# One ring over the attention stage's three PSUM banks and five new ones, and a gain's preparation held back, in a Griffin-style layer on one core

## The chip, the core and the metric

The kernel runs on one core of one Trainium2 chip, as a single launch. The metric is the device time of one execution in microseconds. Before the change it is 1303.85 us, the median of three runs (1301.6 to 1304.78).

## The reference

One layer: a mixer that adds stick-breaking attention and a short gated convolution under two sigmoid gates, and then a convolutional feed-forward network. Both have an RMS norm ahead of them and one behind them. The sequence has 1024 positions, the model 1024 channels, the feed-forward 2816.

```python
h = rms_norm(x, norm_mix_pre)
proj = h @ w_in
q, k, v, cb, cc, cx, g_att, g_conv = jnp.split(proj, IN_SPLITS, axis=-1)
o = stick_breaking_attention(heads(q), heads(k), heads(v))      # 8 heads of 64
y_att = o @ w_att_branch
y_conv = (cb * causal_dwconv(cc * cx, conv_mix_w)) @ w_conv_branch
merged = sigmoid(g_att) * y_att + sigmoid(g_conv) * y_conv
x = x + rms_norm(merged @ w_out, norm_mix_post)

h = rms_norm(x, norm_ffn_pre)
u = causal_dwconv(h @ w_up, conv_ffn_w)
a, g = jnp.split(u, 2, axis=-1)
x = x + rms_norm((gelu(g) * a) @ w_down, norm_ffn_post)
```

## The kernel before

All products are made in half precision with float32 sums. Each operand is split into a high and a low half (L102 on ScalarE writes the high one, L103 on VectorE the low one), and each product is three passes over the pairs of halves. Weights are scaled by a power of two first: ScalarE squares a raw tile and sums it (L63, the `jk_` names), TensorE adds over the partitions with a column of ones (L81, L1419, `pr`), and a few small VectorE steps make the scale from that (L83 to L86, L1414 to L1417).

The layer runs in stages, and each PSUM product takes a bank of a pool:

- **Attention** (to about 407 us), in an order written by hand. Its pools hold eight banks: `pm`, three, for projections and branch products, and a pool of its own for scores and outputs. Branch products made here (`pywc`, L935) are emptied on VectorE by L943.
- **Branches and gates** (410 to 597 us). Attention's pools are closed, and a pool `pz` of eight banks is opened over the same memory. Products of the branches (`pywc`, `pywa`) alternate with those of the gates, one pair of gates per block of 128 channels, d from 1 to 7. A pair is made of seven half-size products in three banks, `pg{d}a`, `pg{d}b` and `pg{d}c` (`Pair.prod`, L2333): several products go one after the other into one bank, and the later ones can only start when the earlier content has been copied out (L2348 and L2353 on ScalarE, L2350, L2357, L2360 and L2362 on VectorE, results `ca`, `cg` and `ug`). The merged activations `ywa` (L1217, L1219) are split into `m16_0` to `m16_7`. In between come loads and squares of `w_down` (`ds`, `jk_dn`: L1314 and L63) and the fetch and split of the next gate's weights (`ws_g`, `wh_g`) and of `w_out` (`ws_wo`, `wh_wo`). The order of this stage on each engine isn't written by hand: it comes from the program's scheduling pass, which knows the pools' banks.
- **Feed-forward** (`ffn`, from about 597 us). Here a planner writes the order of all engines: each step has an engine, a cost, the buffers that it reads and writes and sometimes a due time, and a buffer's `avail` is the planner's time from which steps that touch it may start. The stage begins with the output projection (`py`, L1482: eight tiles of 128 positions in two halves), its norm (L1492 to L1506), the residual, the next norm (L1511) and the transposes (`pt`, L1570). The up-projection follows (L1681, `pu`).

The vector `g_ffn` is the gain of the second norm. It arrives by a DMA at the end of the gates; `gain()` then takes its largest magnitude over the 1024 channels (L1455), makes a power of two of it in four small steps (L199 to L202), and L1458 scales the vector. Before, these steps are ready as soon as the load is. Sums over partitions after attention take their banks from the same pool as the products, by `self.sum_psum`.

Of the kernel before, what the change touches and what calls it, by code (L numbers as in the profile page):

```python
# [44 lines left out]
class Layer:  # L45
    def __init__(self, tc, a):
        self.tc, self.nc, self.a = tc, tc.nc, a
# [232 lines left out]
    def mixer(self, mid):  # L280
        tc, nc, a = self.tc, self.nc, self.a
        hT = self.hp.tile([P, 2, KD, T], F16, tag="hT", name="hT")
        with ExitStack() as ph1:
            pha = ph1.enter_context(ExitStack())
            pm = ph1.enter_context(tc.tile_pool(name="pm", bufs=3, space=bass.MemoryType.PSUM))
            self.sum_psum = (pm, [P, NH], "pm")
            att = pha.enter_context(tc.tile_pool(name="att", bufs=1))
            self.mask = att.tile([P, 2, P], F16, tag="mask", name="mask")
# [884 lines left out]

        self.xp = self.top.enter_context(tc.tile_pool(name="xp", bufs=4))
        self.h7p = self.top.enter_context(tc.tile_pool(name="h7p", bufs=1))
        self.pz = pm = self.top.enter_context(tc.tile_pool(name="pz", bufs=8, space=bass.MemoryType.PSUM))
        self.sum_psum = (pm, [P, NH], "pm")
        m16 = []
        with ExitStack() as ph2:
# [69 lines left out]
            for d in range(1, 8):  # L1249
                p = gp[d]  # L1250
# [44 lines left out]
        gf = self.xp.tile([P, D], F32, tag="x", name="g_ffn")  # L1295
# [22 lines left out]
    dpos, dsums, pz, DIRECT = 0, {}, None, 7  # L1318
# [38 lines left out]
    def ffn(self):  # L1357
        tc, nc, a = self.tc, self.nc, self.a
# [14 lines left out]
        def given(pool, tile):  # L1373
            b = Buf(pool, None)
            b.tile = tile
            pl.caps[pool] = pl.caps[pool] - 1
            b.held = True
            return b
# [7 lines left out]
        def V(cost, fn, r, w, **kw):  # L1386
            return pl.add("V", cost, fn, r, w, **kw)
# [64 lines left out]
        gp, gf = given("x", gpt), given("x", gft)  # L1452

        def gain():
            vec.tensor_reduce(self.g2[:, 0:1], gft, AX.X, ALU.max, apply_absolute_value=True)  # L1455
            self.gain_pow2(self.g2, 2)
        V(1.85, gain, [gf], [gf])
        V(0.74, lambda: vec.tensor_scalar(gft, gft, self.g2[:, 3:4], None, ALU.mult), [], [gf])  # L1458
        xr = {tt: given("ws", t) for tt, t in xrt.items()}
        hn, prods = {}, {}  # L1460
# [607 lines left out]
            pl.emit()  # L2068


class Buf:
    def __init__(self, pool, make):
        self.pool, self.make, self.tile, self.log, self.left, self.avail = pool, make, None, [], 0, 0.0
# [126 lines left out]
class Side:  # L2200
# [19 lines left out]
    def tile(self, name):  # L2220
        self.tiles[name] = self.pm.tile([P, NH], F32, tag="pm", name=name)
        return self.tiles[name]
# [240 lines left out]
```

## Time and profile before

| | |
|---|---|
| median of the runs | 1303.85 us (1303.85, 1304.78, 1301.6) |
| the profiled execution's own time | 1305.79 us |
| its span | 1303.7 us |
| mean granted TensorE clock | 0.999 of full speed |
| TensorE busy | 1284.4 us (99% of the span), 6306 matmuls |
| VectorE busy | 1093.4 us (84%) |
| ScalarE busy | 940.0 us (72%) |
| GpSimd busy | 83.9 us (6%) |
| moved by DMA | 131.52 MB, mean 101 GB/s |

The page gives busy time per engine over the span of one execution; in its rows PE is TensorE, DVE VectorE, ACT ScalarE, POOL GpSimd, and SP the engine that issues most DMAs. A row of a timeline has the start, the duration, the engine, the line of the kernel, the operation, and output and inputs by the program's names (buffer numbers left out, so `cgg` is `cgg4` in the fourth gate). A bracket at its end has the idle time of that engine just before and what ended it.

### The profile page before, as it was taken

Reading aid. Unit: us, or ns where it says so; the run is one execution under the profiler, and the core shown is the slowest. Engines: PE = TensorE matmul, PEld = TensorE weight load, DVE = VectorE, ACT = ScalarE, POOL = GpSimd, SP = SyncE. Lnnn points to the kernel's source line nnn. Section 1 sums busy time; section 2 is a strip of 40 time slices with the busy share of each in tenths; the row PEclk is TensorE's granted clock in tenths of the full one; section 3 lists DMA queues with packets and bytes.
Section 4 is the critical chain, followed back from the end, with each engine's and each line's share of the span. In section 5 each row is a group of like instructions: output and inputs, shape, how many; then the busy total and the mean of one; then the engine's idle time right before and its main releaser. Section 6 shows DMA issues by size and latency. Waiting matters only on the chain.

```text
span 1303.7 us, 16883 instructions
## 1 busy us (share of the span) xinstructions
PE 1284.4 (99%) x6306; PEld 571.0 (44%) x6306; DVE 1093.4 (84%) x1756; ACT 940.0 (72%) x1333; POOL 83.9 (6%) x120
## 2 busy tenths in 40 slices
PE   8999999999999999999999999999999999999997
PEld 4444444444444444444444444444444444444443
DVE  7678888888878967777989999799879979979976
ACT  8478778787778966674666757877966876778534
POOL 2000000000000000000210000100200210120103
PEclk9999999999999999999999999999999999999999
DMA  7511111110101212240695311720961791395707
GB/s 261 130 34 47 52 33 28 38 33 33 50 1 49 66 65 88 90 178 33 155 221 149 113 49 69 278 74 6 199 183 33 117 255 49 53 232 163 200 1 129
DMA packets 68372, 131.52 MB, mean 101 GB/s; under 512 B 36913, under 2 KB 37041, under 8 KB 68290
## 3 DMA queue, kind: packets, MB, share of 16 engines
q1 hardware_dynamic: 57920, 93.74, 23.2%
q0 software_dynamic: 10368, 36.70, 13.7%
q8 instruction: 49, 0.80, 0.2%
q14 instruction: 33, 0.27, 0.1%
q10 hardware_dynamic: 2, 0.00, 0.0%
HBM read 84.52 MB, written 37.78 MB: 94 GB/s over the span
## 4 chain that ended last, share of the span: by engine, by line
PE 83%; DVE 5%; ACT 4%; DMA 4%; issue 2%; POOL 1%; SPq 0%; POOLq 0%; DVEq 0%; ACTq 0%
PE pq L1840 11%; PE py L1482 4%; PE pcb L216 3%; PE pcc L216 3%; PE pcx L216 3%; PE pywa L935 3%; PE pywc L935 3%; PE pk L216 3%; PE pq L216 3%; PE A L963 2%; PE o L963 2%; PE pd L1910 2%; PE z L963 2%; PE pv L413 1%; PE pv L583 1%
## 5 line engine op out<-in xcount | busy, mean ns | idle before, releaser
L1681 PEld LDWEIGHTS <-wh_u 128*128 128x128 f16 x1848 | 179.2, 98 | 218.5 <-issue 1.8
L1431 ACT ACTIVATE wh_u<-ws_u,sc_u 128x1024 f16<-128x1024 f32 (+1 forms) x66 | 66.3, 1007 | 30.2 <-DVE sc_u L1416 9.2
L2333 PEld LDWEIGHTS <-wh_g 128*128 128x128 f16 x588 | 56.9, 98 | 69.8 <-issue 1.7
L1482 PE MATMUL py<-wh_wo,m 128*128 128x512 f16 x384 | 83.4, 379 | 0.9 <-DVE wh_wo L103 0.9
L1433 DVE SCALAR_TENSOR_TENSOR wh_u<-ws_u,sc_u,wh_u 128x1024 f16<-128x1024 f32 (+1 forms) x66 | 72.2, 1103 | 13.9 <-ACT wh_u L1431 13.6
L1844 ACT ACTIVATE st<-pq,sd 128x512 f32<-128x512 f32 x112 | 73.3, 697 | 10.1 <-DVE ua L1724 5.6
L1006 ACT ACTIVATE sh<-sp 128x1024 f16<-128x1024 f32 (+3 forms) x48 | 40.4, 842 | 52.2 <-DVE sp L1001 52.1
L1397 POOL DMA_DIRECT2D acc<-st x56 | 43.2, 772 | 427.3 <-ACT st L1844 425.9
L63 ACT ACTIVATE jk_u<-ws_u 128x1024 bf16<-128x1024 f32 x44 | 46.3, 1052 | 21.0 <-DMA ws_u<-w_up_nt 20.5
L1001 DVE TENSOR_TENSOR sp<-A,sp 1x1024 f32<-1x1024 f32 (+3 forms) x40 | 35.9, 897 | 29.9 <-PE A L963 26.5
L1482 PEld LDWEIGHTS <-m 128*128 128x128 f16 x384 | 37.4, 98 | 46.0 <-issue 1.2
L1713 DVE SCALAR_TENSOR_TENSOR ua<-ca,cw_a,ua 128x1023 f32<-128x1023 f32 (+1 forms) x44 | 56.2, 1278 | 1.3 <-ACT ua L1711 1.2
L1010 DVE TENSOR_TENSOR sh<-sp,sh 128x1024 f16<-128x1024 f32 (+3 forms) x48 | 45.8, 955 | 13.5 <-ACT sh L1006 13.3
L1713 DVE SCALAR_TENSOR_TENSOR ug<-cg,cw_g,ug 128x1023 f32<-128x1023 f32 (+1 forms) x44 | 56.2, 1277 | 0.1
L1036 DVE SCALAR_TENSOR_TENSOR w<-e,w 128x1024 f16<-128x1024 f32 (+3 forms) x48 | 45.8, 953 | 6.8 <-ACT w L1032 6.7
L1032 ACT ACTIVATE w<-e 128x1024 f16<-128x1024 f32 (+3 forms) x48 | 40.5, 844 | 14.8 <-DVE e L1027 13.7
L1027 DVE TENSOR_TENSOR e<-e,g 128x1024 f32<-128x1024 f32 (+3 forms) x48 | 45.7, 952 | 2.5 <-ACT g L1023 2.5
L982 ACT ACTIVATE e<-z,cz 128x1024 f32<-128x1024 f32 (+3 forms) x48 | 43.1, 897 | 6.3 <-PE z L963 6.3
L996 ACT ACTIVATE sp<-e,one 128x1024 f32<-128x1024 f32 (+3 forms) x48 | 44.4, 925 | 4.0 <-DVE e L991 2.7
L216 PE MATMUL pcb<-hT,wh_cb 128*128 128x512 f16 x192 | 45.1, 380 | 0.0
L216 PE MATMUL pcx<-hT,wh_cx 128*128 128x512 f16 x192 | 44.9, 379 | 0.0
L216 PE MATMUL pcc<-hT,wh_cc 128*128 128x512 f16 x192 | 44.6, 380 | 0.0
(777 smaller groups left out, 2984.6 us busy)
## 6 DMA issues: line engine op xcount, KB each, us to landing
acc<-st POOLq DMA_DIRECT2D x56, 512.0 KB, 6.4
ws_u<-w_up_nt SPq DMA_DIRECT2D x44, 512.0 KB
ds<-w_down SPq DMA_DIRECT2D x22, 512.0 KB
ws_g<-w_in_nt SPq DMA_DIRECT2D x14, 512.0 KB
x<-x SPq DMA_DIRECT2D x8, 512.0 KB
ws_wo<-w_out SPq DMA_DIRECT2D x8, 512.0 KB
xr<-x SPq DMA_DIRECT2D x8, 512.0 KB
yacc<-acc SPq DMA_DIRECT2D x16, 256.0 KB
```

Source lines behind the costliest of these rows:

```text
L63: self.nc.scalar.activation(self.junk(f"jk_{name}"), src, AF.Square, accum_out=acc)
L216: nc.tensor.matmul(ps, w[:, wi, ds(k * P, P)], hT[:, hi, k, ds(c * NH, NH)], start=n == 0, stop=n == last)
L935: nc.tensor.matmul(ps, w[0][:, wi, ds((d % 2) * NH + k * P, P)], acts[bi][k][:, hi, ds(c * NH, NH)], start=n == 0, stop=n == 11)
L963: nc.tensor.matmul(out, w, mv, skip_group_check=True, **kw)
L1431: A(C["As" if big else "Ash"], lambda: act.activation(dst.t[:, 0, dsl], src.t[:, ssl], AF.Copy, scale=sb.t["s"]), [(src, sreg), sb], [(dst ...
L1433: V(C["V" if big else "Vh"], lambda: vec.scalar_tensor_tensor(dst.t[:, 1, dsl], src.t[:, ssl], sb.t["s"], dst.t[:, 0, dsl], ALU.mult, ALU. ...
L1482: pe.matmul(b.t, m16[k].t[:, h_, ds(tt * P, P)], wo[k].t[:, w_, sl], start=k == 0 and p == 0, stop=k == 7 and p == 2)
L1681: pe.matmul(b.t, p.w[wt].t[:, wi, ds(wc * NH + k * P, P)], pr.block(i, h, k), start=first and n == 0, stop=n == 3 * KH - 1, skip_group_che ...
L1713: V(C["V"], lambda lag=lag: vec.scalar_tensor_tensor(u.t[:, lag:], c.t[:, :T - lag], sm.t[:, 2 - lag:3 - lag], u.t[:, lag:], ALU.mult, ALU ...
L1840: pe.matmul(b.t, fa[p].t[:, h, ds(fo * NH + tt * P, P)], wa[p].t[:, x, ds(wo * NH, NH)], start=first and n == 0, stop=n == 5, skip_group_c ...
L1844: A(C["Ah"], lambda tt=tt, b=b, st=st: act.activation(st.t[:, tt % 2, :], b.t, AF.Copy, scale=q.sd.t[:, 0:1]), [b, q.sd], [(st, str(tt % 2 ...
L2333: nc.tensor.matmul(ps, w[wt][:, wi, ds(wc * NH + k * P, P)], self.block(i, hi, k), start=first and n == 0, stop=n == 3 * KH - 1, skip_grou ...
```

## The change

The pool `pm` of three banks, opened in the attention stage, is opened on the layer's own stack, so that it isn't closed with attention. Where a new pool of eight banks was opened, one of five is opened now, and `Ring` hands out banks in turn: five of the new pool, then the three of the old. Everything later that asked `pz` for a bank asks the ring. Second, in the feed-forward's list `gain` is given an extra buffer that is available from 17.0 us of the planner's time on.

```diff
-            pm = ph1.enter_context(tc.tile_pool(name="pm", bufs=3, space=bass.MemoryType.PSUM))
+            pm = self.top.enter_context(tc.tile_pool(name="pm", bufs=3, space=bass.MemoryType.PSUM))
+            self.pm3 = pm
...
-        self.pz = pm = self.top.enter_context(tc.tile_pool(name="pz", bufs=8, space=bass.MemoryType.PSUM))
+        self.pz = pm = Ring((self.top.enter_context(tc.tile_pool(name="pz", bufs=5, space=bass.MemoryType.PSUM)), 5),
+                            (self.pm3, 3))
...
-        V(1.85, gain, [gf], [gf])
+        late = note()
+        late.avail = 17.0
+        V(1.85, gain, [gf, late], [gf])
...
+class Ring:
+    def __init__(self, *pools):
+        self.order, self.n = [p for p, k in pools for _ in range(k)], 0
+
+    def tile(self, *a, **kw):
+        p = self.order[self.n % len(self.order)]
+        self.n += 1
+        return p.tile(*a, **kw)
```

No engine has another number of matmuls, activations or vector steps. The order is the same up to the last product of the attention stage. From there to about 620 us it differs; three places follow. Lines after the change are numbered 1 to 16 higher.

TensorE at the end of attention, rows that only repeat left out: the last product of the branch's seventh block, first its last weight load, then the first products after it. Before:

```order
L935 LDWEIGHTS wh_wc3_0_3823
L935 MATMUL pywc7_1_3962<-p16_3_3740,wh_wc3_0_3823 128x512
L935 LDWEIGHTS wh_wc0_0_3858
L935 MATMUL pywc0_0_4033<-p16_0_3714,wh_wc0_0_3858 128x512
L935 MATMUL pywc0_0_4033<-p16_1_3716,wh_wc0_0_3858 128x512
```

After:

```order
L936 LDWEIGHTS wh_wc3_0_3823
L936 MATMUL pywc7_1_3962<-p16_3_3740,wh_wc3_0_3823 128x512
L936 LDWEIGHTS wh_wc0_0_3858
L936 MATMUL pywc1_0_4096<-p16_0_3714,wh_wc0_0_3858 128x512
L936 MATMUL pywc1_0_4096<-p16_1_3716,wh_wc0_0_3858 128x512
```

The first product in the banks of the next stage was pywc0_0 and is pywc1_0, which takes a bank of the pool that stays open.

ScalarE at the third gate (`cgg3` and `ugg3` are the copies of `pg3a` and `pg3c`, `wh_g4` the fourth gate's weights, `jk_dn0` the first square of `w_down`). Before:

```order
L102 ACTIVATE m16_1_4834<-ywa1_4290,sc7_4822 128x1024
L2348 ACTIVATE cgg3_4851<-pg3a_4837 128x512
L102 ACTIVATE m16_2_4978<-ywa2_4322,sc7_4822 128x1024
L102 ACTIVATE wh_g4_0_4876<-ws_g4_0_4702,sc8_4867 128x1024
L102 ACTIVATE wh_g4_1_4877<-ws_g4_1_4706,sc8_4867 128x1024
L102 ACTIVATE wh_g4_2_4878<-s12_g4_4786,sc8_4867 128x1024
L2353 ACTIVATE ugg3_4928<-pg3c_4915 128x512
L63 ACTIVATE jk_dn0_4984,sm_dn0_4981<-ds0_4982 128x1024
L2375 ACTIVATE cag3_4850<-pg3a_4837,sc_g3_4942 128x512
```

After:

```order
L102 ACTIVATE m16_1_4833<-ywa1_4289,sc7_4821 128x1024
L102 ACTIVATE m16_2_4977<-ywa2_4321,sc7_4821 128x1024
L2364 ACTIVATE cgg3_4850<-pg3a_4836 128x512
L2369 ACTIVATE ugg3_4927<-pg3c_4914 128x512
L102 ACTIVATE wh_g4_0_4875<-ws_g4_0_4701,sc8_4866 128x1024
L102 ACTIVATE wh_g4_1_4876<-ws_g4_1_4705,sc8_4866 128x1024
L102 ACTIVATE wh_g4_2_4877<-s12_g4_4785,sc8_4866 128x1024
L63 ACTIVATE jk_dn0_4983,sm_dn0_4980<-ds0_4981 128x1024
L2391 ACTIVATE cag3_4849<-pg3a_4836,sc_g3_4941 128x512
```

The copy of `pg3a` has moved behind `m16_2`, and that of `pg3c` ahead of the fourth gate's weights. TensorE's order moves with it: between `pr` (now 31 matmuls after the start of the product `pg2b` ahead of it, before 12) and the second product into `pg3a` there are now 17 matmuls and another `pr`, where before there were 36; and ahead of the last product into `pg4b` there are 7 matmuls fewer.

VectorE at the end of the gates (`cgg7` is the seventh gate's, `sc12` the scale of `w_out`). Before:

```order
L103 SCALAR_TENSOR_TENSOR m16_6_5504<-ywa6_4618,sc7_4822,m16_6_5504 128x1024
L1455 TENSOR_REDUCE g_ffn_5643<-g_ffn_5641 128x1
L199 TENSOR_SCALAR g_ffn_5643<-g_ffn_5643 128x1
L200 TENSOR_SCALAR g_ffn_5643<-g_ffn_5643 128x1
L201 TENSOR_SCALAR g_ffn_5643<-g_ffn_5643 128x1
L202 TENSOR_SCALAR g_ffn_5643<-g_ffn_5643 128x1
L2357 TENSOR_TENSOR cgg7_5485<-pg7b_5507,cgg7_5485 128x512
L83 TENSOR_SCALAR sc12_5594<-pr13_5598 128x1
```

After, where those steps stand now, behind the scale of the first up-projection weights (`sc_u0`) and ahead of these weights' low half and of the norm's first steps:

```order
L1419 TENSOR_SCALAR sc_u0_5733<-sc_u0_5733 128x1
L1457 TENSOR_REDUCE g_ffn_5642<-g_ffn_5640 128x1
L199 TENSOR_SCALAR g_ffn_5642<-g_ffn_5642 128x1
L200 TENSOR_SCALAR g_ffn_5642<-g_ffn_5642 128x1
L201 TENSOR_SCALAR g_ffn_5642<-g_ffn_5642 128x1
L202 TENSOR_SCALAR g_ffn_5642<-g_ffn_5642 128x1
L1435 SCALAR_TENSOR_TENSOR wh_u0_0_5772<-ws_u0_0_5379,sc_u0_5733,wh_u0_0_5772 128x1024
L1496 SCALAR_TENSOR_TENSOR hn0_5794<-py0_0_5669,sgn_549,g_post_5638 128x512
```

Nothing of `g_ffn` is left between `m16_6` and `cgg7`. L1458, the scaling of the vector, has moved to just ahead of the residual's first step, L1506 (L1510 after), and the three matmuls of `pr_u0` stand 9 matmuls earlier in the output projection.

## The prediction

> **What bounds the kernel now.** I read the head of the page first, then the list of what TensorE waited for, then busy time by stretches, and last the timelines around each wait that the edits touch.
>
> The first two rows are the span and TensorE's share of it; then the longest waits of TensorE in the list of waits (total, count, longest) that lie between attention and the up-projection; then TensorE's busy time in three stretches of 100, 50 and 400 us, with its granted clock as the number after the brackets.
>
> ```profile
> span 1303.7 us, 16883 instructions
> PE 1284.4 (99%) x6306; PEld 571.0 (44%) x6306; DVE 1093.4 (84%) x1756; ACT 940.0 (72%) x1333; POOL 83.9 (6%) x120
> ...
> PE pu2a L1681 <- ACT cg L1690: 1.7, 1, 1.7
> ...
> PE pu0b L1681 <- DVE ca L1687: 1.1, 1, 1.1
> PE pg7b L2333 <- DVE cgg L2357: 1.0, 1, 1.0
> PE pywc L935 <- DVE ywc L943: 0.9, 1, 0.9
> PE py L1482 <- DVE wh_wo L103: 0.9, 1, 0.9
> PE pt L1570 <- DVE hn L1511: 0.6, 1, 0.6
> ...
> 450.00:550.00 100.00, 100.00 (x471) 1.00 0.22 74
> ...
> 700.00:750.00 50.00, 47.78 (x223) 1.00 0.40 119
> 800.00:1200.00 400.00, 400.00 (x1875) 1.00 0.53 134
> ```
>
> TensorE is the bound: it is idle for 1303.7 − 1284.4 = 19.3 us in the whole span, and not at all from 800 to 1200 us. The change removes no matmul, so the only time that it can give back is idle time, and the six waits shown add up to 6.3 us. What can be lost is open: from 450 to 550 us, the stage of the gates, TensorE is busy in every microsecond, so any wait that a new order brings there is paid in full. One matmul costs 400 / 1875 = 0.2133 us of TensorE when nothing waits.
>
> A difference of 0.3%, 3.9 us, is about the least that a measurement of this kernel can tell from none. The profiled execution took 1305.79 us with a span of 1303.7; the median of the runs is 1303.85. Terms below are differences against the trace, and I set them against the median.
>
> **The boundary after attention.** The timeline of DVE and TensorE there, with start, duration, engine, line, and in brackets the idle time before and what ended it:
>
> ```profile
> 404.32 0.75 DVE L943 TENSOR_SCALAR ywc<-pywc,sgn 128x512 f32<-128x512 f32 x1 [0.58 <-PE pywc L935]
> ...
> 405.67 2.10 PE L935 MATMUL pywc<-p,wh_wc 128*128 128x512 f16 x9
> ...
> 407.92 0.74 DVE L943 TENSOR_SCALAR ywc<-pywc,sgn 128x512 f32<-128x512 f32 x1
> ...
> 408.72 2.55 PE L935 MATMUL pywc<-p,wh_wc 128*128 128x512 f16 x11 [0.95 <-DVE ywc L943]
> ```
>
> Before, the old three-bank pool is handed over as a whole, so the first product after it waits for the last eviction of the old one (407.92 + 0.74 = 408.66) although it uses another bank. After, that product (pywc1_0) sits in a kept bank whose last content left at 404.32 + 0.75 = 405.07, while TensorE is not there until 407.77. The wait of 0.95 goes, with 2.7 us to spare. The next product (pywc0_0) goes to a bank of the new pool, 2.6 us later. Term: **−0.9**.
>
> **g_ffn's preparation held back.** The same view at the end of the gates:
>
> ```profile
> 593.10 0.17 PE L81 MATMUL pr<-rb,ones 128*128 128x1 bf16 x1
> ...
> 594.41 1.22 DVE L1455 TENSOR_REDUCE g_ffn<-g_ffn 128x1 f32<-128x1024 f32 x1 [1.25 <-DMA g_ffn<-g_ffn_pre]
> ...
> 596.11 0.14 DVE L202 TENSOR_SCALAR g_ffn<-g_ffn 128x1 int32<-128x1 int32 x1
> 596.17 0.68 DVE L2357 TENSOR_TENSOR cgg<-pg7b,cgg 128x512 f32<-128x512 f32 x1
> ...
> 596.90 2.75 PE L2333 MATMUL pg7b<-hT,wh_g 128*128 128x512 f16 x12 [1.02 <-DVE cgg L2357]
> ...
> 597.63 0.14 DVE L86 TENSOR_SCALAR sc<-sc 128x1 int32<-128x1 int32 x1
> ...
> 597.75 0.74 DVE L1458 TENSOR_SCALAR g_ffn<-g_ffn 128x1024 f32<-128x1024 f32 x1
> 598.31 2.17 ACT L102 ACTIVATE wh_wo<-ws_wo,sc 128x1024 f16<-128x1024 f32 x2
> ...
> 599.48 2.48 DVE L103 SCALAR_TENSOR_TENSOR wh_wo<-ws_wo,sc,wh_wo 128x1024 f16<-128x1024 f32 x2
> ...
> 600.82 1.02 PE L1482 MATMUL py<-wh_wo,m 128*128 128x512 f16 x4 [0.95 <-DVE wh_wo L103]
> ```
>
> DVE stands before L1455 for the DMA of g_ffn, then runs it and its four small steps, and the eviction of pg7b (L2357) stands behind them until 596.17. It could start when pg7b's product is done, which is just before pr at 593.10, so at about 593.3. TensorE wants the bank at 596.90 − 1.02 = 595.88, and the eviction would be done at 594.0. Term: **−1.0**. The scale of w_out (L83 to L86, done at 597.77) stands behind the same stretch, as its input pr is done at 593.27. Without it ScalarE's first wh_wo starts some 3 us earlier, and DVE's first L103, now done at 600.72, at about 597.9; TensorE, itself 1 us earlier, needs it at 598.9. Term: **−0.95**. What ends last there then is TensorE itself.
>
> The moved work is 1.22 + 4 × 0.14 + 0.74 = 2.5 us of DVE. The order puts the first 1.8 us behind L1417 and L1458 ahead of L1506. What stands there now:
>
> ```profile
> 618.94 0.16 DVE L1414 TENSOR_SCALAR sc_u<-pr_u 128x1 int32<-128x1 int32 x1 [4.60 <-PE pr_u L1419]
> ...
> 624.24 2.48 DVE L1506 SCALAR_TENSOR_TENSOR x<-hn,r_post,xr 128x1024 f32<-128x1024 f32 x2 [0.20 <-POOL r_post L1503]
> ...
> 673.96 1.09 PE L1570 MATMUL pt<-ident,hn 128*128 128x128 f32 x8 [0.63 <-DVE hn L1511]
> ```
>
> DVE idles 4.60 us ahead of L1414 for the sums of pr_u, and the order has these on TensorE 9 matmuls, 1.9 us, earlier. The preparation is paid from that, and the work in front of L1506 ends up between 0 and 2.5 us later. Queued behind it on DVE are the four L1492, which empty the banks of the first out-projections, and L1506; the first TensorE wait in their line is pt's 0.63 us, 50 us later. Bound: 0 to +2.5 if nothing between absorbs it. I take **0**, because the 4.60 us is idle time nearest to it. That g_ffn's DMA is waited for no longer costs nothing: it had landed at 594.4.
>
> **The gates in another order.** This is the cost side, and the larger uncertainty: the pools' banks decide the order, and from 410 to 597 us TensorE, DVE and ScalarE run the same work in another one. At the third gate, second product into pg3a comes after fewer other matmuls, and ScalarE's eviction L2348 of the first now stands behind three L102 of m16 in place of two. Rows of before:
>
> ```profile
> 504.74 2.75 PE L2333 MATMUL pg2b<-hT,wh_g 128*128 128x512 f16 x12
> ...
> 507.46 0.16 PE L81 MATMUL pr<-rb,ones 128*128 128x1 bf16 x1
> ...
> 509.69 2.17 ACT L102 ACTIVATE m<-ywa,sc 128x1024 f16<-128x1024 f32 x2
> ...
> 511.77 0.57 ACT L2348 ACTIVATE cgg<-pg3a 128x512 f32<-128x512 f32 x1
> ...
> 513.47 1.15 ACT L102 ACTIVATE m<-ywa,sc 128x1024 f16<-128x1024 f32 x1 [1.13 <-DVE ywa L1219]
> ```
>
> In the new order pr comes 31 matmuls after the start at 504.74: 504.74 + 31 × 0.2133 − 0.95 = 510.4. The scale takes about 1.1 us on DVE, then ScalarE runs 2.17 + 1.15 + 0.57 to L2348's end: 511.5 + 3.9 = 515.4. TensorE comes to the second pg3a after 48 matmuls and two pr: 504.74 + 10.24 + 0.3 − 0.95 = 514.35. A wait of **+1.0**, where before there was none. The evictions of the third gate's other banks give 0.15 more by the same count.
>
> The fourth gate hangs on a longer chain, through loads into slots that ScalarE frees:
>
> ```profile
> 516.62 2.98 SPq L1314 DMA_DIRECT2D ds<-w_down  x2
> ...
> 518.12 1.04 ACT L63 ACTIVATE jk_dn<-ds 128x1024 bf16<-128x1024 f32 x1
> ...
> 525.53 1.06 ACT L63 ACTIVATE jk_dn<-ds 128x1024 bf16<-128x1024 f32 x1 [3.21 <-DMA ds<-w_down]
> ...
> 540.91 1.06 ACT L63 ACTIVATE jk_g<-ws_g 128x1024 bf16<-128x1024 f32 x1 [1.96 <-DMA ws_g<-w_in_nt]
> ...
> 543.13 1.29 DVE L103 SCALAR_TENSOR_TENSOR m<-ywa,sc,m 128x1024 f16<-128x1024 f32 x1 [0.69 <-ACT m L102]
> ...
> 544.34 0.68 DVE L2357 TENSOR_TENSOR cgg<-pg4b,cgg 128x512 f32<-128x512 f32 x1
> ...
> 545.55 0.81 PE L2333 MATMUL pg4b<-hT,wh_g 128*128 128x512 f16 x3
> ```
>
> The fourth load of w_down can only be issued once the first jk_dn has freed its slot; its issue ends at 516.62 + 2.98 = 519.60 and it is used at 525.53, 5.9 us on. The new order puts the first jk_dn behind L2348 (to 515.4), one more eviction of its size (0.57) and three L102 (2.17 + 1.15): it starts at 519.3 in place of 518.12, so the fourth is 1.2 us late too. On the way to m16_3 ScalarE waits 1.96 us more for a load, whose slot hangs only partly on that chain; I take a third of the delay, 0.4 us, as left when L2357 ends (0 to 1.2 is possible): 545.02 + 0.4 = 545.4. TensorE has 7 matmuls fewer ahead of the last pg4b: 545.55 − 7 × 0.2133 − 0.95 + 1.15 = 544.26. A wait of **+1.1**. Bounds for the whole stage: 0, if neither chain is as late as worked out, to 4, if the later gates, whose filler is cut by 0 to 3 matmuls, each bring a further half microsecond.
>
> The Trainium skill's page "DMA: Bandwidth & Descriptors" (section on the anatomy of one DMA) fits a transfer's time as about 2.0 us plus its bytes at 436 GB/s, which is an estimated 3.2 us for these 512 KB. By it the fourth load would not be what ScalarE waits for, the wait of 1.1 would fall away and the sum would be 1302.0. The trace does not agree: 5.9 us from the end of its issue.
>
> **Sum.** −0.9 − 1.0 − 0.95 + 0 + 1.0 + 0.15 + 1.1 = −0.6 us; 1303.85 − 0.6 = **1303.2 us**.
>
> **Rivals.**
>
> *Faster: the gates cost nothing.* DVE and ScalarE both reach their evictions in time, and the passage is smoother than before: −2.85, and of the three later waits (1.7, 1.1 and 0.6, together 3.4) some go as well because the out-projection starts earlier. Over 0.3% is reached once 1.05 of those 3.4 go; at most 1303.85 − 6.2 = 1297.6. For it: the gates' waits come out of sums of a few tenths. Against: the moved work lies on DVE just ahead of that line. Chance 0.20.
>
> *Slower: the delay of ScalarE's loads is carried through the gates.* Each later gate's weights are loaded into slots that the one before frees, so the 1.1 us at pg4b may come again at pg5b, pg6b and pg7b, and the loads of w_out, behind the same slots, then keep the waits at pg7b and at py. Then −0.9 + 1.15 + 4 × 1.1 = +4.65, 1308.5 us. It decides from 3.9 us, that is once the gates cost 4.8 with both late waits kept, or 6.75 with both gone. For it: ScalarE waited for a load 3.21 and 1.96 us there already. Against: those 1.96 us were mostly absorbed in my chain. Chance 0.20.
>
> *It does not do what it says.* The boundary's wait is met again within the gates by the next bank, and the late waits are replaced by TensorE waiting for w_out's weights: no difference, 1303 to 1305. Against: the eviction is 2.7 us early. Chance 0.12.
>
> **The numbers.** The forecast has 0.48, with a range of its own from 1301.0 (the gates at 0) to 1306.5 (the gates at 4, 1.5 of the moved work's 2.5 us not covered: 1301.0 + 4 + 1.5). Forecast and the case of no difference make "within 0.3%": 0.60. The range from 1299.2 to 1308.2 leaves out the far part of either rival, 0.08 and 0.10.
>
> **What would show it.** In the list of TensorE's waits of after: pywc behind L943, pg7b and py gone; new rows of about 1 us at pg3a behind ScalarE's L2348 (now L2364) and at pg4b behind DVE's L2357 (L2373); pt at 674 us still about 0.6. TensorE's busy time from 450 to 550 should fall from 100.00 to about 97.8. If it stays at 100 the gates' part is wrong, and if pt's or pu2a's wait is over 2 us longer, the moved work was not covered.

## The result, and the profile after

| | before | after |
|---|---|---|
| median of 13 runs each, side by side | 1304.77 us | 1301.97 us |
| ratio to before | | 0.9984, 95% interval 0.9977 to 0.9992 |
| profiled execution: its time, its span | 1305.79, 1303.7 us | 1304.68, 1302.9 us |

By the ratio the change makes the kernel 2.1 us faster (1.0 to 3.0 by the interval); the two medians alone differ by 2.8 us, which lies inside that. The forecast was 0.6 us faster.

Head of the page of the changed kernel, its list of TensorE's waits (total, count, longest) for this part, and TensorE's busy time in the three stretches shown of before:

```profile
span 1302.9 us, 16883 instructions
PE 1285.9 (99%) x6306; PEld 572.5 (44%) x6306; DVE 1093.6 (84%) x1756; ACT 941.1 (72%) x1333; POOL 84.0 (6%) x120
...
PE pu2a L1685 <- ACT cg L1694: 1.2, 1, 1.2
PE pu0b L1685 <- DVE ca L1691: 1.1, 1, 1.1
PE pg3a L2349 <- ACT cgg L2364: 1.1, 1, 1.1
...
PE pt L1574 <- DVE hn L1515: 0.4, 1, 0.4
...
450.00:550.00 100.00, 98.95 (x465) 1.00 0.24 74
700.00:750.00 50.00, 48.63 (x227) 1.00 0.40 116
800.00:1200.00 400.00, 400.00 (x1876) 1.00 0.53 134
```

The three waits at pywc, pg7b and py are gone from the list. One has come: pg3a, 1.05 us in the timeline, which is the whole loss of the stretch from 450 to 550 (100.00 to 98.95). No wait at pg4b stands in the list. So between 400 and 620 us TensorE lost 2.92 us before and 1.05 after. From 800 to 1200 nothing changed.

The timelines of after at the four places, in order of time. At the boundary:

```profile
406.97 3.40 PE L936 MATMUL pywc<-p,wh_wc 128*128 128x512 f16 x15
...
409.23 0.74 DVE L944 TENSOR_SCALAR ywc<-pywc,sgn 128x512 f32<-128x512 f32 x1
```

TensorE goes on without a break (the row shows the 15 matmuls that start before 410 us, the last six of them of the next product), while the last eviction of the old stage only starts at 409.23.

At the third and fourth gate:

```profile
512.78 3.23 ACT L102 ACTIVATE m<-ywa,sc 128x1024 f16<-128x1024 f32 x3 [2.81 <-DVE sc L85]
...
514.25 1.24 PE L2349 MATMUL pg3c<-hB,wh_g 128*128 128x512 f16 x5
...
515.33 6.17 SPq L1316 DMA_DIRECT2D ds<-w_down  x4
...
515.92 0.57 ACT L2364 ACTIVATE cgg<-pg3a 128x512 f32<-128x512 f32 x1
...
516.54 2.75 PE L2349 MATMUL pg3a<-hT,wh_g 128*128 128x512 f16 x12 [1.05 <-ACT cgg L2364]
...
524.69 1.06 ACT L63 ACTIVATE jk_dn<-ds 128x1024 bf16<-128x1024 f32 x1 [0.76 <-DMA ds<-w_down]
...
543.06 0.68 DVE L2373 TENSOR_TENSOR cgg<-pg4b,cgg 128x512 f32<-128x512 f32 x1
...
545.08 0.38 PE L2349 MATMUL pg5b<-hB,wh_g 128*128 128x512 f16 x1
...
545.30 1.89 PE L2349 MATMUL pg4b<-hT,wh_g 128*128 128x512 f16 x8
```

ScalarE runs three L102 in a row (3.23 us) ahead of the copy of pg3a, and TensorE waits for that copy. At the fourth gate the eviction ends at 543.74, 1.6 us ahead of TensorE. The row of the queue (SPq) has the issues of four loads of w_down: the fourth ends at 515.33 + 6.17 = 521.50, and the load is used at 524.69.

At the end of the gates and in the output projection:

```profile
594.52 0.69 DVE L2373 TENSOR_TENSOR cgg<-pg7b,cgg 128x512 f32<-128x512 f32 x1 [2.12 <-PE pr L81]
...
596.93 2.75 PE L2349 MATMUL pg7b<-hT,wh_g 128*128 128x512 f16 x12
...
599.52 2.75 PE L1486 MATMUL py<-wh_wo,m 128*128 128x512 f16 x12
...
615.92 0.16 DVE L1416 TENSOR_SCALAR sc_u<-pr_u 128x1 int32<-128x1 int32 x1 [3.22 <-PE pr_u L1421]
```

VectorE now idles ahead of pg7b's eviction, which is done 1.7 us before TensorE needs the bank, and it still idles 3.22 us ahead of L1416, behind which the held-back work now stands.

### The profile page after: what moved, and what is told of

Its sections match the earlier page's. It is cut to its first block, busy times and chain, and to the rows that moved or that the text cites. A ratio compares the mean times of both kernels' runs of the same rounds, so it can differ in the third digit from the quotient of the medians.

```text
span 1302.9 us, 16883 instructions
## 1 busy us (share of the span) xinstructions
PE 1285.9 (99%) x6306; PEld 572.5 (44%) x6306; DVE 1093.6 (84%) x1756; ACT 941.1 (72%) x1333; POOL 84.0 (6%) x120
```

## The experiments

Two theories went in. **W**: each wait of TensorE between 400 and 620 us is paid in full, and they add up. **R**: the handed-over banks carry the gain. Ratios are to runs of the kernel before on the same chip.

**The ring alone.**

```diff
-        late = note()
-        late.avail = 17.0
-        V(1.85, gain, [gf, late], [gf])
+        V(1.85, gain, [gf], [gf])
```

> The ring alone, without the held-back gain; the gates' order is that of the changed kernel. Theory W (every wait of TensorE between 400 and 620 us is paid in full, and the waits add up): the wait at the boundary (0.95 us, L943) is gone, the wait of 1.05 at pg3a behind ScalarE's copy is there, the waits at pg7b (1.0) and py (0.95) are back: -0.95 + 1.05 = +0.1 us, no difference from the kernel before. Theory R (the handed-over banks carry the gain): 2 us faster, whatever stands at pg7b and py.

Measured: 0.9999 (0.9990 to 1.0008). The timeline of TensorE's waits up to 620 us:

```profile
514.96 2.75 PE L2347 MATMUL pg3a<-hT,wh_g 128*128 128x512 f16 x12 [1.03 <-ACT cgg L2362]
599.11 18.07 PE L1484 MATMUL py<-wh_wo,m 128*128 128x512 f16 x83 [0.80 <-DVE wh_wo L103]
```

The boundary's wait is gone, pg3a's is there, py's is back. Pg7b's is not, in this execution; more on that below. The ring gains 0.95 and loses 1.03, and the median shows no gain: R falls.

**The held-back gain alone**, the same edit the other way, in the kernel before.

> The held-back gain alone, with the old pools; the gates' order is that of the kernel before. Theory W: the boundary keeps its 0.95, pg3a has no wait, pg7b (1.0) and py (0.95) lose theirs: -1.97 us, 0.9985 of the kernel before, as good as the whole change. Theory R: no difference.

Measured: 0.9982 (0.9973 to 0.9991), as good as the whole change. Up to 620 us its TensorE waits once:

```profile
407.31 5.35 PE L935 MATMUL pywc<-p,wh_wc 128*128 128x512 f16 x24 [0.95 <-DVE ywc L943]
```

Both medians are as W has them. The second profile of the kernel before, below, limits what that shows of the late waits.

**m16_2 split one gate later**, in the changed kernel. In the first version the output projection gets blocks 2 and 3 of `m16` in each other's place; the second puts them right, with the same order of instructions.

```diff
                 if d == 3:
-                    split_m(2, ms[2])
                     self.dn_sums(GROUPS[0])
+                if d == 4:
+                    split_m(2, ms[2])
...
-                m16.append(t)
+                m16.insert(d, t)
```

> The changed kernel with the split of m16_2 moved behind the third gate, so that two L102 and not three stand ahead of the copy of pg3a on ScalarE. Theory W: the copy ends 1.1 us earlier, the wait of 1.05 at pg3a is gone, and the time is 1.0 us below the changed kernel's, 2.9 us or 0.9978 of the kernel before, if the fourth gate, which now has the split, gets no wait. Rival S (the delay only moves on: the split stands ahead of the fourth gate's eviction instead): about 1 us of wait at pg4b, and the changed kernel's time.

> The same order as the run with m16_2 behind the third gate, but with the blocks of m16 handed to the output projection in their right places. Theory W: as there, no wait at the boundary, at pg3a, pg7b and py, 0.2 us at pg6c: 0.9979 of the kernel before, 1 us below the changed kernel. Rival S: the time of the changed kernel, 0.9985.

Measured: 0.9979 (0.9969 to 0.9989) for the first, 0.9983 (0.9975 to 0.9992) for the second. In both profiles pg3a's wait is gone. TensorE's waits in the gates are 0.25 us in the first profile, and in the second

```profile
574.59 2.75 PE L2350 MATMUL pg6b<-hB,wh_g 128*128 128x512 f16 x12 [0.28 <-DVE cag L2367]
581.07 2.75 PE L2350 MATMUL pg6c<-hT,wh_g 128*128 128x512 f16 x12 [0.93 <-ACT ugg L2370]
```

So the three L102 do cause the wait at pg3a. Whether the 1 us is kept, the two runs leave open: both intervals hold W's 0.9978 and the changed kernel's 0.9984.

**The ring turned, and turned with the later split.**

```diff
-        self.pz = pm = Ring((self.top.enter_context(tc.tile_pool(name="pz", bufs=5, ...)), 5),
-                            (self.pm3, 3))
+        self.pz = pm = Ring((self.pm3, 3),
+                            (self.top.enter_context(tc.tile_pool(name="pz", bufs=5, ...)), 5))
```

> The changed kernel with the ring turned: the three kept banks first, the five new ones behind. The first product after attention goes into the first kept bank, and the gates' order differs again in places, with three L102 ahead of the copy of pg3a as in the changed kernel. Theory W: no wait at the boundary, about 1.05 at pg3a, none at pg7b and py: the changed kernel's time within 0.5 us, 0.9984 of the kernel before. Rival O (which bank comes first matters): the kept bank's own last eviction, 0.7 us later than that of the others, brings back part of the boundary's wait, up to 0.95.

> The changed kernel with both variants: the kept banks first in the ring and m16_2 split behind the third gate, its blocks in their right places. Theory W: no wait at the boundary and at pg3a, none over 0.3 at the later gates: 2.9 us below the kernel before, 0.9978, the best so far. Rival S: the split, now ahead of the fourth gate's sigmoids, brings waits of about 1 us at gates 4 to 6 as at pg6c in the run before: 0.9984.

Measured: 0.9987 (0.9978 to 0.9997) and 0.9984 (0.9975 to 0.9993). Neither has a wait at the boundary, so rival O falls. The second has no wait at all from 400 to 680 us, and then this one:

```profile
692.99 4.10 PE L1686 MATMUL pu2a<-hA,wh_u 128*128 128x512 f16 x12 [2.29 <-ACT hb L1616]
```

W's 0.9978 did not come: part of what was saved ahead is given back in the up-projection, behind ScalarE. More is lost there than the wait: the 12 matmuls behind it took 4.10 us. The ring turned alone has a shorter wait at that place, 1.77 us, and its 12 matmuls took 2.75. The stretch from 680 to 720 us, first with the later split and then without it, shows the granted clock at 0.96 and at 1.00:

```profile
680.00:720.00 40.00, 35.97 (x167) 0.96 0.38 106
```

```profile
680.00:720.00 40.00, 36.15 (x173) 1.00 0.44 122
```

None of these versions is shown to be faster than the held-back gain alone.

**The moved work doubled.**

```diff
             vec.tensor_reduce(self.g2[:, 0:1], gft, AX.X, ALU.max, apply_absolute_value=True)
+            vec.tensor_reduce(self.g2[:, 0:1], gft, AX.X, ALU.max, apply_absolute_value=True)
```

> The changed kernel with L1457, the reduction of g_ffn, done twice in its new place: 1.2 us more of VectorE ahead of wh_u and of the four L1496. Theory C (the idle time ahead of L1416 and the 50 us up to the first transposes cover it): no change against the changed kernel, 0.9984 of the kernel before, and pt's wait at 672 us stays near 0.4. Rival U (the moved work lies open): 1.2 us more, pt's wait at 1.6, 0.9993 of the kernel before.

Measured: 0.9991 (0.9983 to 1.0000), which leaves both open. The one profile, of the fastest of its runs, speaks for C: VectorE idles ahead of L1416 as in the changed kernel and then runs both,

```profile
613.15 0.16 DVE L1416 TENSOR_SCALAR sc_u<-pr_u 128x1 int32<-128x1 int32 x1 [3.23 <-PE pr_u L1421]
...
613.47 1.21 DVE L1457 TENSOR_REDUCE g_ffn<-g_ffn 128x1 f32<-128x1024 f32 x1
614.72 1.22 DVE L1458 TENSOR_REDUCE g_ffn<-g_ffn 128x1 f32<-128x1024 f32 x1
```

and pt has no wait at all. Rival U needed 1.6 us there. The second profile of the changed kernel has none at pt either, so in such an execution 1.2 us more are covered; for the slower executions the run leaves it open.

**The fourth load of w_down crowded.**

```diff
-            nc.sync.dma_start(t, self.a["w_down"][f])
+            go = nc.sync.dma_start(t, self.a["w_down"][f])
+            if f == 3:
+                pool = self.top.enter_context(self.tc.tile_pool(name="idle", bufs=1, space=bass.MemoryType.DRAM))
+                with self.tc.issue_after(go.ins):
+                    nc.sync.dma_start(pool.tile([P, D], F32, tag="idle", name="idle"), self.a["w_down"][f])
```

> The changed kernel with one transfer more: a copy of 512 KB within the chip's memory issued on the same queue right behind the fourth load of w_down, read by nobody. Theory L (that load took 5.9 us in the kernel before and 3.2 in the changed one because before another transfer is issued 0.1 us behind it, and after only 1.1 us later): the load is used some 2 to 3 us after where it is now, the chain of ScalarE to the last eviction of pg4b, which has 1.5 us to spare, is late by about 1, and TensorE gets the wait at pg4b that was forecast: about +1 us, 0.9992 of the kernel before. Rival N (the load's length has another reason): it stays at 3 to 4 us, no wait at pg4b, the changed kernel's time.

Measured: 0.9984 (0.9975 to 0.9993). The four issues of w_down, the fourth use, and the fourth gate's eviction:

```profile
513.62 6.16 SPq L1316 DMA_DIRECT2D ds<-w_down  x4
...
525.21 1.06 ACT L63 ACTIVATE jk_dn<-ds 128x1024 bf16<-128x1024 f32 x1 [2.46 <-DMA ds<-w_down]
...
543.08 0.68 DVE L2377 TENSOR_TENSOR cgg<-pg4b,cgg 128x512 f32<-128x512 f32 x1
...
543.37 0.38 PE L2353 MATMUL pg5b<-hB,wh_g 128*128 128x512 f16 x1
...
543.82 2.53 PE L2353 MATMUL pg4b<-hT,wh_g 128*128 128x512 f16 x11
```

The load took 5.4 us from the end of its issue (519.78) to its use, in place of 3.2, as theory L had it; that is one execution, and below the same load varies about as much with no edit at all. The eviction then ended at 543.76, and TensorE started on the bank at 543.82. The list of waits shows none there, but that start is 0.45 us behind the start of the matmul ahead of it, 0.22 in the changed kernel: the time to spare was used up and some 0.2 us were lost, in place of L's 1. Counted from the second product into pg3a (514.83 here, 516.54 in the changed kernel) the load's use is 2.2 us later and the eviction's end 1.7. But a few rows also changed places in this version (one square of weights, `jk_g`, stands behind three L102 on ScalarE now), so the 1.7 is not shown to be the load's alone.

**The kernel before with g_ffn's load first, and both kernels once more.** This edit separates VectorE's wait for the load from its work:

```diff
+        gf = self.xp.tile([P, D], F32, tag="x", name="g_ffn")
+        nc.gpsimd.dma_start(gf, a["g_ffn_pre"].broadcast_to([P, D]))
         gp = self.xp.tile([P, D], F32, tag="x", name="g_post")
         nc.gpsimd.dma_start(gp, a["g_mix_post"].broadcast_to([P, D]))
-        gf = self.xp.tile([P, D], F32, tag="x", name="g_ffn")
-        nc.gpsimd.dma_start(gf, a["g_ffn_pre"].broadcast_to([P, D]))
```

> The kernel before with g_ffn's load issued ahead of that of g_post, some 2.2 us earlier; the planner then puts its reduction, its four steps and also L1458 ahead of L2357, the first ones even ahead of the split of m16_6. Theory Q (what costs is that VectorE's queue has this work ahead of L2357): L2357 starts 0.4 us later than now though no load is waited for, the waits at pg7b and py are 1.4 and 1.3 in place of 1.0 and 0.95: 0.5 to 0.9 us slower than before. Rival D (what costs is the wait of 1.25 for the load): pg7b's and py's waits are gone and the time is 1.9 us below the kernel before.

> The kernel before with g_ffn's load first, once more: its first profile had no wait at pg7b and py (rival D), but its median was that of the kernel before. Rival D alone gives 0.9985 and the same picture in the second profile. If the load's landing varies from one execution to the next (V), the second profile has part of the waits at pg7b and py back, and the median stays between 0.9985 and 1.

> The kernel before once more, for a second profile of it: executions of one kernel differ by up to 5 us, and the sum of the prediction rests on one of them. Theory W: the waits at the boundary (0.95), at pg7b (1.0) and at py (0.95) are there within 0.3 us, and what differs lies at the start (the loads of the first 50 us) and from 660 us on. Rival V (these waits themselves come and go): one of them is gone or doubled.

> The changed kernel once more, for a second profile. Theory W: 1.05 at pg3a, none at the boundary, pg7b and py. Rival V: the wait at pg3a differs by over 0.3, or one at pg7b or py has come back.

Measured: the load first gives 0.9998 (0.9989 to 1.0007) and 1.0001 (0.9990 to 1.0012). Its two profiles differ: no wait at pg7b and py in the first, 0.20 and 0.94 in the second. So neither theory holds: D's 1.9 us are not in the median, and Q's longer waits are in neither profile. The second profile of the kernel before, of an execution of 1301.65 us, has these waits in this part:

```profile
407.65 5.35 PE L935 MATMUL pywc<-p,wh_wc 128*128 128x512 f16 x24 [0.95 <-DVE ywc L943]
597.82 18.07 PE L1482 MATMUL py<-wh_wo,m 128*128 128x512 f16 x83 [0.25 <-DVE wh_wo L103]
```

The boundary's 0.95 is the same, but pg7b and py have 0 and 0.25 where the first profile had 1.02 and 0.95. The second profile of the changed kernel (1300.36 us) has 1.03 at pg3a and nothing else up to 620 us, as the first. So rival V is right for the late waits alone: without the held-back gain they come and go, and pt's wait behind them does too. The waits at pg7b, py and pt together are 2.60 and 0.25 us in the two profiles of the kernel before, 0 and 2.52 in the two with the load first, and 2.30 with the ring alone (0.80 at py, 1.50 at pt). In the nine profiles with the gain held back pg7b and py never wait, and pt waits 0.42 at most.

What varies with them is the fourth load of w_down. The four issues and the fourth use, in the second profile of the kernel before, in that of the held-back gain alone, and in the second one with the load first; all three have the same order of issues there:

```profile
512.44 6.10 SPq L1314 DMA_DIRECT2D ds<-w_down  x4
...
521.91 1.06 ACT L63 ACTIVATE jk_dn<-ds 128x1024 bf16<-128x1024 f32 x1 [0.93 <-DMA ds<-w_down]
```

```profile
512.09 6.10 SPq L1314 DMA_DIRECT2D ds<-w_down  x4
...
524.27 1.06 ACT L63 ACTIVATE jk_dn<-ds 128x1024 bf16<-128x1024 f32 x1 [3.35 <-DMA ds<-w_down]
```

```profile
512.12 6.10 SPq L1314 DMA_DIRECT2D ds<-w_down  x4
...
524.05 1.06 ACT L63 ACTIVATE jk_dn<-ds 128x1024 bf16<-128x1024 f32 x1 [3.08 <-DMA ds<-w_down]
```

From the end of the issues to the use that is 3.4, 6.1 and 5.8 us, and it was 5.9 in the first profile of before. Where the load was long and the gain not held back, pg7b and py waited, 1.97 us in the first profile of before and 1.14 in the second with the load first; where it was short (3.4 and 3.5 us), they waited 0.25 and 0. With the gain held back neither waited, though the load took 6.1 us. That fits a late load making the gates late on VectorE, these freeing g_ffn's slot late, and g_ffn's steps then standing in front of pg7b's eviction. In the first profile of before GpSimd issues g_ffn's load at 589.71, 0.8 us ahead of pg7b's product (590.51), in the second at 586.79, 2.6 us ahead of it (589.40). It would also explain why loading g_ffn earlier did not help the median, and holding its steps back did: the second takes VectorE's queue out of that chain whenever the load lands. It is argued from these executions and not shown by an edit. The ring alone fits it for pg7b only: its load took 3.9 us and pg7b did not wait, but py waited 0.80 all the same, and why is open.

## Why the prediction was right, and where it was off

The direction was right, 1301.97 us lies in the range, and "within 0.3%", to which 0.60 was given, came true. The size was not right: −2.1 us was measured (−1.0 to −3.0), −0.6 forecast. By its steps:

- **The boundary, −0.9: right.** 0.95 us in each profile with the old pools that was read for it, 0 in each with the ring.
- **The late waits, −1.0 and −0.95: right as to what goes, and only one execution's as to size.** They are gone in both profiles of after and in those of the other versions with the gain held back. In the kernel before they were 1.97 us in one execution and 0.25 in another; the prediction rests on the first. The held-back gain alone measured −2.3 us (−1.2 to −3.5).
- **The moved work, 0: right** in the profiles: pt's wait went from 0.63 to 0.40 in the first profiles and was 0 in both second ones, and with the work doubled it was 0 too. The 4.60 us of idle time stand ahead of the moved work and could not pay for it; what did is that pr_u's sums come earlier: the scale starts at 615.92 in place of 618.94, in part through the time saved ahead, and L1496, behind the moved work, starts at 619.34, where L1492 started at 619.60.
- **pg3a, +1.0: right**, 1.05 and 1.03. The copy ended at 516.49 behind three L102, as worked out.
- **The third gate's other banks, +0.15: not there.**
- **pg4b, +1.1: the step that failed.** It took the 5.9 us of the fourth load of w_down as a fixed price and moved it along with the first jk_dn. The first jk_dn did move, from 518.12 to 520.00, but the fourth use came at 524.69, earlier than before's 525.53, since the load took 3.2 us. By the fit of the Trainium skill's page "DMA: Bandwidth & Descriptors" (the section on the anatomy of one DMA), an estimated 3.2 us, that wait would not come: so it was, though the page gives the fit for transfers issued by GpSimd and this load is issued by SP, and ScalarE still waited 0.76 us for it. The trace that I set against it was one execution of a load that takes 3.4 to 6.1 us in that order. (The sum by the fit is 1302.15, not 1302.0.) The crowded run, with a load of 5.4 us, lost some 0.2 us there: the chain from the load to the bank is there, but how much of a delay it passes on stays open.

Without the failed term and the 0.15, and with the measured 1.05, the sum is −1.8, near the middle of the interval. That is luck in part: with the 0.25 of the second profile in place of the late waits' 1.95, it would be −0.1. The interval of 1.0 us to either side also shows that less than 0.3% can be told from none, which the prediction took for the least.

Of the rivals, the faster one (1297.6) had its first half in part: of the gates' three added waits one came. Its second half did not: the waits from 660 to 720 us added up to 3.4 us in the first profile of before and 3.5 in that of after (2.6 in both second ones). The slower one, the load's delay carried through the gates, did not come, for the same reason that pg4b's wait did not. That the change does nothing holds for one half of it: the ring gives 0.95 and takes 1.03.

## What to carry to other kernels

A stall that hangs on a load has no one length: look at a second execution before its wait is summed as a fixed price, and prefer taking a step out of the queue in front of the bottleneck to loading its input earlier, since the first works whenever the load lands. A pool that stays open saves the wait of its handover, but where a scheduler places work by banks it reorders everything behind, so read the new order for the copy that a reused bank waits for. Two edits made together are worth pulling apart: here one carried the whole gain, as far as the intervals tell, and the other only paid for itself.

## What the runs showed of the hardware that was not expected

- The same load of 512 KB, in the same place of the same order of issues, took 3.4 us in one execution of the kernel before and 5.9 in another, and 3.5, 5.8 and 6.1 in the other three profiles with that order. Where the next issue stood 1.2 us behind it (the changed kernel), it took 3.2 and 3.9.
- The two profiled executions of the kernel before differ by 4.1 us in span (1303.7 and 1299.6), more than the change is worth. TensorE's first wait, for g_row at the start, was 3.4 and 2.3 us. The two are 1.1 us apart at the boundary after attention (408.72 and 407.65), 3.0 at the output projection (600.82 and 597.82) and 4.1 at pu2a (701.16 and 697.02), so the rest came with the late waits and between the output projection and pu2a, where pt's 0.63 is the longest wait that only one of them has. From 720 to 1200 us both are busy throughout.
- Behind a wait of 2.29 us at pu2a TensorE's granted clock read 0.65 from 692.9 to 697.2 us, and 12 matmuls took 4.10 us; behind 1.77 us at the same place it read 1.00, and they took 2.75. That is one execution of each.
